# The entry of a fused encoder step: a smaller first chunk, the norm weight spread by TensorE, other loads and a written-out order

## Chip, core and metric

The kernel runs on one core of a Trainium2 chip. The core has TensorE (PE in the profile: matrix products, and transposes as products with an identity matrix), VectorE (DVE), ScalarE (ACT), GpSimd (POOL) and SyncE (SP, which here only issues loads and stores). Each engine takes its own instructions one after the other in a fixed order and waits for the others through counters (semaphores); ScalarE issues loads too. The metric is device time of one execution in microseconds (us).

## What is computed

One inference step of a hybrid encoder layer, for 1,024 prompt tokens and 32 sample tokens, 1,024 wide. Only its first part matters here: the norm of the tokens and the combined projection, whose columns feed three mixers (mLSTM, stick-breaking attention, S5).

```python
def layer(x, mem_k, mem_v, past_k, past_v, c0, n0, m0, s0_re, s0_im, conv_prev, prm):
    h = rmsnorm(x, prm['ln_mix_g'])
    z = h @ prm['w_in'] + prm['b_in']
    q_a, k_a, v_a, o_a, i_a, f_a, q_b, k_b, v_b, u_c = split_cols(z)
    ...
    x = x + y_mix @ prm['w_out']
    x = x + cross_attn(rmsnorm(x, prm['ln_x_g']), mem_k, mem_v, prm['w_xq'], prm['w_xo'])
    f, conv_new = conv_ffn(rmsnorm(x, prm['ln_ffn_g']), prm, conv_prev)
    ...
```

## The kernel before

**Split products.** Every f32 product is made of three on rounded operands (type fp32r): high part of the weights with high and low part of the tokens, low part of the weights with the high part of the tokens. The high part of a tile is a copy by ScalarE with rounding, the low part the difference, by VectorE or GpSimd.

**Token tiles.** `x_tile(i)` makes the normalised and transposed tokens of tile i, 128 tokens (tile 8 has the 32 of the sample). Its generator `norm_T` records: ScalarE squares and sums the tile; VectorE scales the sum and GpSimd takes its power -1/2; VectorE multiplies the tile by it and by the norm weights `gmix`, which must stand in all 128 partitions; and twice, for each half of the 1,024 columns: TensorE transposes four blocks into a PSUM tile `tp`, ScalarE copies it into `h_hi` (za and zb are the zones of `h_lo` and `h_hi`), VectorE makes the low part in `h_lo`.

**Projection.** `W` streams the weight tiles of 128 columns: `load` brings 512 KB, `split` makes `w_hi` and `w_lo`. The first three weight tiles are u0 and u1 (input of S5) and the gate, which has its high and low part side by side in one tile (zone zr) and so 16 products a chunk, where the others have 24. `dense_cmajor` runs these three chunk by chunk over the tokens (0 to 383, 384 to 767, 768 to 1055), so that TensorE has work before all tokens are there; `need_h(c)` holds a chunk back until its tiles are recorded. From the fourth weight tile on `dense` runs each tile over all chunks. `ev_in` evacuates each result by ScalarE.

**Order.** The Python code records instructions in the order of its own clock model, with side work (`vec_late` for later vectors, `s5`, `mlstm`, `stick`, the norm of the memory tokens) recorded between the products. A scheduler of the framework then sets each engine's order by its own estimate, within the dependences. It also gives every load one of eight counters; an issue waits until the load that had the counter before has landed. The first loads are issued by SyncE in this order, ahead of the bias vectors and the rest:

```python
        x_load(0, sy)
        sy.dma_start(gmix, a["ln_mix_g"][0].partition_broadcast(P))
        x_load(1, sy)
        x_load(2, sy)
        W.load()
        x_load(3, sy)
        W.load()
```

All instructions pass through one helper, so that the profile shows nearly all at line 173; tiles are told apart by names: zf and zy hold the loaded tokens and small vectors, mm is the PSUM tile of a product, gp one of small work.

Of the kernel before, what the change touches and what calls it, by code (L numbers as in the profile page):

```python
# [8 lines left out]
F32R = mybir.dt.float32r  # L9
# [31 lines left out]
IN_AT = [0, 3 * P, 6 * P, TA]  # L41


IN_W = max(IN_AT[c + 1] - IN_AT[c] for c in range(NCH))

# [8 lines left out]
def tile_fn(tc, *args):  # L54
# [77 lines left out]
    class Timed:  # L132
# [23 lines left out]
        def __getattr__(self, name):  # L156
# [17 lines left out]
            return timed  # L174

# [85 lines left out]
    with ExitStack() as top:  # L261
# [122 lines left out]
        class WStream:  # L384
# [21 lines left out]
            def split(self):  # L406
# [124 lines left out]
        sp = Bag({"ss": (4, 8), "stg": (3, IN_W), "sthl": (2, 2 * IN_W, "R"), "nat": (1, 9 * P)})  # L531
# [22 lines left out]
        def norm_T(src_ap, n, gB, hi, lo, t0, xt=None):  # L554
# [7 lines left out]
            s.activation(sq[:n], xt[:n].rearrange("p (k c) -> p k c", k=KD), AF.Square, accum_out=ss[:n, 0:1])  # L562
            yield
            v.tensor_scalar(ss[:n, 1:2], ss[:n, 0:1], 1.0 / D, EPS, op0=ALU.mult, op1=ALU.add)
            g.tensor_tensor(out=ss[:n, 2:3], in0=ss[:n, 1:2], in1=mhalf[:n], op=ALU.pow)
            yield
            v.scalar_tensor_tensor(xt[:n], xt[:n], ss[:n, 2:3], gB[:n], op0=ALU.mult, op1=ALU.mult)
            yield
            for q in range(2):
                ps = tp()  # L570
                for j in range(4):
                    k = 4 * q + j
                    pe.transpose(ps[:, j, :n], xt[:n, k * P:(k + 1) * P], ident[:n, :n])
                s.activation(hi[:, 4 * q:4 * q + 4, t0:t0 + n], ps[:, :, :n], AF.Copy)
                v.tensor_tensor(out=lo[:, 4 * q:4 * q + 4, t0:t0 + n], in0=ps[:, :, :n],
                                in1=asf(hi[:, 4 * q:4 * q + 4, t0:t0 + n]), op=ALU.subtract)
                yield
# [9 lines left out]
        def x_tile(i):  # L587
            yield from norm_T(None, P if i < 8 else TS, gmix, h_hi, h_lo, i * P, xts[i])
# [24 lines left out]
        sy.dma_start(bgate[0:4, :], a["b_in"][0, 1536:1540].unsqueeze(1))  # L613
        sy.dma_start(bgate[32:36, :], a["b_in"][0, 1540:1544].unsqueeze(1))
# [22 lines left out]
        def vec_late():  # L637
# [10 lines left out]
            yield  # L648
            pa, pb = gp(), gp()
            pe.transpose(pa[:, :34], ra[:34], ident[:34, :34])  # L650
            pe.transpose(pb[:, :88], rb, ident[:88, :88])
# [60 lines left out]
        def ev_in(jj, c, ps):  # L712
            key, j = order[jj]
            sl = slice(IN_AT[c], IN_AT[c + 1])
            w = IN_AT[c + 1] - IN_AT[c]
            rs_ = slice(j * P, (j + 1) * P)
            pv = ps[:, :w]
            if key == "u":
                if c == 0:
                    full[jj] = xb.tile([P, 8, NB], "ur")  # L720
                n0, nn = IN_AT[c] // 8, w // 8
# [8 lines left out]
            if key == "gate":  # L730

                sl_ = sp.tile([P, 3 * P], "stg")[:, :w]
# [16 lines left out]
            if key in ("qb", "kb"):  # L749
                hl = sp.tile([P, 2, IN_W], "sthl", F32R)[:, :, :w]  # L750
# [7 lines left out]
            if key in ("kb", "vb", "va", "oa"):  # L758
# [915 lines left out]

        hm = lambda k, c: (h_hi[:, k, IN_AT[c]:IN_AT[c + 1]], h_lo[:, k, IN_AT[c]:IN_AT[c + 1]])
        in_n = [IN_AT[c + 1] - IN_AT[c] for c in range(NCH)]
        chunks = list(range(NCH))
        h_free = []
        xw_ = add(Window((x_tile(i) for i in range(9)), 4))
        until(lambda: xn[0] >= 1)  # L1680
        W.prime(1)

        def need_h(c):
            until(lambda: xn[0] * P >= min(IN_AT[c + 1], T) and (c < 2 or xn[0] == 9))
# [19 lines left out]
        main = dense_cmajor(3, hm, chunks, in_n, ev_in, need_h)  # L1704
# [805 lines left out]
```

## Time and profile before

| | us |
|---|---|
| median of 3 runs | 1724.47 (1716.87 to 1728.94) |
| profiled execution | 1717.52 |
| its span, first to last instruction | 1715.7 |
| TensorE busy in the span | 1639.6 (96%) |

The span is what the rows below are counted from; 1.8 us lie around it. A timeline row has the start, the duration, the engine (q for its sequencer, which issues loads), line, operation, tiles, shapes, the number of merged instructions, and in brackets the idle time of the engine before it and what ended it. The end of a product is modelled, so that its duration overlaps that of the next; the pitch of their starts tells how fast they run.

### The profile page before, as it was taken

The numbers are of one execution on the slowest core, as the hardware profiler recorded it, in microseconds if no ns is written. First come the engines' busy times: TensorE is split into PE (matmuls) and PEld (weight loads), VectorE is DVE, ScalarE is ACT, GpSimd is POOL, SyncE is SP. The second block draws the span as 40 slices with busy tenths as digits, with TensorE's granted clock in tenths as the row PEclk, the third lists the DMA queues.
The fourth block names the chain that finished last, engine by engine and source line by source line (L and its number), as shares of the span: only waits on it lengthen the run. The fifth ranks groups of instructions, "written<-read, shape, count | busy, mean of one in ns | idle before, by whom it ended". The sixth has DMA issues, their size and how long they took to land.

```text
span 1715.7 us, 30436 instructions
## 1 busy us (share of the span) xinstructions
PE 1639.6 (96%) x11616; PEld 1595.5 (93%) x11616; DVE 1137.6 (66%) x2221; ACT 754.9 (44%) x1480; POOL 456.2 (27%) x612
## 2 busy tenths in 40 slices
PE   5999999999999899999999889999999999999997
PEld 5999989998899799999998889999999998999997
DVE  6788878745786657766656678877777777233232
ACT  5434534634665554544444534444444445111143
POOL 5234425011213333201102554333333330000022
PEclk9999999999999999999999989999999999999999
DMA  7464544254579874456653555322222227332111
GB/s 216 145 179 109 128 109 106 77 157 136 142 231 268 235 226 136 139 160 183 182 162 112 156 156 160 98 88 81 75 76 75 76 74 259 96 100 75 45 67 65
DMA packets 328391, 229.90 MB, mean 134 GB/s; under 512 B 43564, under 2 KB 309707, under 8 KB 327991
## 3 DMA queue, kind: packets, MB, share of 16 engines
q1 hardware_dynamic: 309991, 214.57, 42.6%
q10 hardware_dynamic: 18256, 13.40, 2.7%
q8 instruction: 92, 1.51, 0.4%
q14 instruction: 52, 0.43, 0.1%
HBM read 170.95 MB, written 56.38 MB: 133 GB/s over the span
## 4 chain that ended last, share of the span: by engine, by line
PE 76%; DVE 9%; DMA 9%; ACT 2%; issue 2%; POOL 2%; SPq 1%; ACTq 0%; DVEq 0%; POOLq 0%
PE mm L173 47%; PE gp L173 19%; PE tp L173 10%; DVE zy L173 3%; DVE zf L173 2%; DVE zx L173 2%; DMA out_dram<-zf 2%; DVE zr L173 1%; DVE w_lo L173 1%; POOL zf L173 1%; DMA zf<-d_act 1%; SPq L173 1%; POOL zy L173 1%; DMA d_mv<-zr 1%; DMA zf<-d_e 1%
## 5 line engine op out<-in xcount | busy, mean ns | idle before, releaser
L173 PE MATMUL mm<-zb,w_hi 128*128 128x352 f32 (+4 forms) x1234 | 365.2, 329 | 2.7 <-DVE zb L173 1.3
L173 PE MATMUL mm<-zr,w_hi 128*128 128x352 f32 (+2 forms) x1358 | 289.9, 313 | 6.3 <-DVE zx L173 2.8
L173 ACT ACTIVATE w_hi<-w_raw 128x1024 fp32r<-128x1024 f32 (+1 forms) x150 | 149.6, 997 | 284.8 <-PE mm L173 203.8
L173 PE MATMUL mm<-zb,w_lo 128*128 128x384 f32 (+2 forms) x826 | 272.4, 330 | 0.0
L173 POOL TENSOR_TENSOR zf<-zf 128x352 f32<-128x352 f32 (+5 forms) x98 | 117.4, 1200 | 578.4 <-ACT zf L173 493.2
L173 PE MATMUL mm<-zr,w_lo 128*128 128x264 f32 (+2 forms) x1058 | 236.2, 304 | 0.7 <-ACT zf L173 0.7
L173 PEld LDWEIGHTS mm<-zb,w_hi 128*128 128x128 f32 x1234 | 226.4, 189 | 4.7 <-DVE zb L173 1.6
L173 PEld LDWEIGHTS mm<-zr,w_hi 128*128 128x128 f32 x1358 | 217.2, 192 | 8.3 <-DVE zx L173 3.1
L173 DVE TENSOR_TENSOR w_lo<-w_raw,w_hi 128x1024 fp32r<-128x1024 f32 (+1 forms) x127 | 160.4, 1263 | 54.9 <-ACT w_hi L173 54.2
L173 DVE TENSOR_TENSOR zx<-mm,zx 128x352 f32<-128x352 f32 (+3 forms) x120 | 62.7, 523 | 186.1 <-PE mm L173 184.3
L173 PE MATMUL mm<-za,w_hi 128*128 128x384 f32 (+1 forms) x552 | 183.1, 332 | 0.0
L173 PEld LDWEIGHTS mm<-zr,w_lo 128*128 128x128 f32 x1058 | 164.7, 189 | 0.9 <-ACT zf L173 0.9
L173 PEld LDWEIGHTS mm<-zb,w_lo 128*128 128x128 f32 x826 | 156.5, 190 | 0.7
L173 PE MATMUL tp<-ident,zf 128*128 128x128 f32 (+3 forms) x530 | 89.2, 286 | 28.6 <-DVE zf L173 20.6
L173 PE MATMUL mm<-zy,w_hi 128*128 128x352 f32 x456 | 113.1, 324 | 1.6 <-DVE zx L173 1.6
L173 PE MATMUL gp<-zy 128*128 128x132 f32 (+13 forms) x722 | 109.8, 290 | 3.1 <-DVE zg L173 2.4
L173 DVE TENSOR_TENSOR zy<-zy 128x16 f32<-128x16 f32 (+9 forms) x371 | 97.3, 303 | 16.3 <-POOL zy L173 7.7
L173 ACT ACTIVATE zf<-gp 128x512 f32<-128x512 f32 (+6 forms) x180 | 75.6, 476 | 73.9 <-PE gp L173 57.1
L173 PEld LDWEIGHTS mm<-za,w_hi 128*128 128x128 f32 x552 | 105.6, 191 | 0.5
L173 PEld LDWEIGHTS gp<-zy 128*128 128x128 f32 (+6 forms) x722 | 97.3, 186 | 5.4 <-DVE zg L173 2.6
L173 PEld LDWEIGHTS tp<-ident,zf 128*128 128x128 f32 (+3 forms) x530 | 64.7, 146 | 38.2 <-DVE zf L173 19.2
L173 POOL TENSOR_TENSOR zy<-zy 128x16 f32<-128x16 f32 (+8 forms) x123 | 82.5, 682 | 64.4 <-DVE zy L173 54.6
(232 smaller groups left out, 3358.7 us busy)
## 6 DMA issues: line engine op xcount, KB each, us to landing
w_raw<-in_w_ffn_a_dram SPq DMA_DIRECT2D x27, 512.0 KB
w_raw<-in_w_out_dram SPq DMA_DIRECT2D x24, 512.0 KB
w_raw<-in_w_xq_dram SPq DMA_DIRECT2D x24, 512.0 KB
w_raw<-in_w_xo_dram SPq DMA_DIRECT2D x24, 512.0 KB
w_raw<-in_w_in_dram SPq DMA_DIRECT2D x23, 512.0 KB
d_act<-zx SPq DMA_DIRECT2D x22, 528.0 KB
zf<-d_act SPq DMA_DIRECT2D x22, 528.0 KB
w_raw<-in_w_ffn_down_dram SPq DMA_DIRECT2D x16, 512.0 KB
```

The lines of the kernel that those rows point to most:

```text
L173: return f(*args, **kw)
```

## The change

- The first three weight tiles run over chunks of 256, 384 and 416 tokens (`IN_FIRST`), the others over 384, 384 and 288 as before.
- The norm weight comes as one row of 4 KB through ScalarE's queue; two f32 products with a row of ones spread it over the partitions, and VectorE copies the result into `gmix`.
- The first weight tile is loaded ahead of token tile 2; bias and later vectors are issued by ScalarE (`rows`, `bgate`).
- `norm_T` multiplies each half of the columns right before that half's transposes.
- `pin` ties an instruction to the last pinned one of its engine, so that pinned instructions keep the order in which they are recorded. All ScalarE and VectorE instructions of `x_tile` and of the first three weight splits are pinned. The low parts of these splits go from GpSimd to VectorE.
- Tiles 0 and 1 are recorded by a written-out sequence; the transposes of `vec_late` wait for 8 us of the model's clock and keep the recorded order.

```diff
+IN_FIRST = [0, 2 * P, 5 * P, TA]
...
+    def pin(eng, name, *args, **kw):
+
+        if eng.key in pinned:
+            with tc.issue_after(pinned[eng.key]):
+                r = getattr(eng, name)(*args, **kw)
+        else:
+            r = getattr(eng, name)(*args, **kw)
+        pinned[eng.key] = r.ins
...
-                s.activation(hi[:, :kt, :cols], raw[:, :kt, :cols], AF.Copy)
-                (v if self.at + len(self.ready) > 2 else g).tensor_tensor(
-                    out=lo[:, :kt, :cols], in0=raw[:, :kt, :cols], in1=asf(hi[:, :kt, :cols]), op=ALU.subtract)
+                do = pin if self.at + len(self.ready) < 3 else free
+                do(s, "activation", hi[:, :kt, :cols], raw[:, :kt, :cols], AF.Copy)
+                do(v, "tensor_tensor", out=lo[:, :kt, :cols], in0=raw[:, :kt, :cols], in1=asf(hi[:, :kt, :cols]),
+                   op=ALU.subtract)
...
-            v.scalar_tensor_tensor(xt[:n], xt[:n], ss[:n, 2:3], gB[:n], op0=ALU.mult, op1=ALU.mult)
-            yield
             for q in range(2):
+                xh = xt[:n, 512 * q:512 * q + 512]
+                do(v, "scalar_tensor_tensor", xh, xh, ss[:n, 2:3], gB[:n, 512 * q:512 * q + 512], op0=ALU.mult,
+                   op1=ALU.mult)
                 ps = tp()
                 for j in range(4):
                     k = 4 * q + j
                     pe.transpose(ps[:, j, :n], xt[:n, k * P:(k + 1) * P], ident[:n, :n])
-                s.activation(hi[:, 4 * q:4 * q + 4, t0:t0 + n], ps[:, :, :n], AF.Copy)
-                v.tensor_tensor(out=lo[:, 4 * q:4 * q + 4, t0:t0 + n], in0=ps[:, :, :n],
-                                in1=asf(hi[:, 4 * q:4 * q + 4, t0:t0 + n]), op=ALU.subtract)
+                do(s, "activation", hi[:, 4 * q:4 * q + 4, t0:t0 + n], ps[:, :, :n], AF.Copy)
+                do(v, "tensor_tensor", out=lo[:, 4 * q:4 * q + 4, t0:t0 + n], in0=ps[:, :, :n],
+                   in1=asf(hi[:, 4 * q:4 * q + 4, t0:t0 + n]), op=ALU.subtract)
                 yield
...
+        grow = xts[7][0:1, :]
+        s.dma_start(grow, a["ln_mix_g"][0].unsqueeze(0))
         x_load(0, sy)
-        sy.dma_start(gmix, a["ln_mix_g"][0].partition_broadcast(P))
         x_load(1, sy)
+        W.load()
         x_load(2, sy)
         W.load()
         x_load(3, sy)
-        W.load()
+        for q in range(2):
+            pq = gp()
+            pe.matmul(pq, ones4[0:1, :], grow[:, 512 * q:512 * q + 512], start=True, stop=True)
+            v.tensor_copy(gmix[:, 512 * q:512 * q + 512], pq)
...
-        xw_ = add(Window((x_tile(i) for i in range(9)), 4))
-        until(lambda: xn[0] >= 1)
+
+        first = [x_tile(i) for i in range(2)]
+        for x in first:
+            next(x)
+            next(x)
+        for _ in first[0]:
+            pass
+        next(first[1])
         W.prime(1)
+        for _ in first[1]:
+            pass
+        add(Window((x_tile(i) for i in range(2, 9)), 2))
```

VectorE's first instructions before, from its first one on: SCALAR_TENSOR_TENSOR is the multiplication of a tile, TENSOR_TENSOR za the low part of a half (tp with its number is the half), TENSOR_SCALAR zf a tile's statistic.

```order
L173 TENSOR_SCALAR zf_87<-zf_87 128x1
L173 TENSOR_SCALAR zy_91<-zy_91 128x128
L173 SCALAR_TENSOR_TENSOR zf_87<-zf_87 128x1024
L173 TENSOR_TENSOR zy_91<-zy_91,ident_114 16x256
L173 TENSOR_SCALAR zf_87<-zf_87 128x1
L173 SCALAR_TENSOR_TENSOR zf_87<-zf_87 128x1024
L173 TENSOR_SCALAR zf_87<-zf_87 128x1
L173 TENSOR_TENSOR za_75<-tp_193,zb_79 128x4x128
L173 SCALAR_TENSOR_TENSOR zf_87<-zf_87 128x1024
```

VectorE with the change, from tile 0's first low part (tp_190) to the second weight tile's low part; 64x256, 128x128 and 16x256 are operations of S5 on loaded parameters, the last of them on `ssm_d`.

```order
L175 TENSOR_TENSOR za_75<-tp_190,zb_79 128x4x128
L175 SCALAR_TENSOR_TENSOR zf_87<-zf_87 128x512
L175 TENSOR_TENSOR za_75<-tp_198,zb_79 128x4x128
L175 SCALAR_TENSOR_TENSOR zf_87<-zf_87 128x512
L175 TENSOR_TENSOR za_75<-tp_206,zb_79 128x4x128
L175 TENSOR_TENSOR w_lo_214<-w_raw_130,w_hi_213 128x1024
L175 SCALAR_TENSOR_TENSOR zf_87<-zf_87 128x512
L175 TENSOR_SCALAR zy_91<-zy_91 64x256
L175 TENSOR_SCALAR zy_91<-zy_91 128x128
L175 TENSOR_TENSOR zy_91<-zy_91,ident_114 16x256
L175 TENSOR_TENSOR za_75<-tp_218,zb_79 128x4x128
L175 TENSOR_TENSOR w_lo_230<-w_raw_133,w_hi_229 128x1024
```

Before, two tiles are multiplied ahead of the first low part; now multiplication and low part of a half take turns, and S5's operations stand ahead of tile 1's last low part.

ScalarE around the same place with the change: zb is the copy of a transposed half, DMA a load that it issues; the three last rows ahead of w_hi_229 are two S5 loads and the copy of tile 1's second half.

```order
L175 ACTIVATE zb_79<-tp_198 128x4x128
L175 DMA zy_91<-in_ffn_conv_w_dram 22x128
L175 DMA zy_91<-in_ffn_conv_b_dram 22x128
L175 DMA zy_91<-in_ssm_c_im_dram 128x64
L175 ACTIVATE zb_79<-tp_206 128x4x128
L175 ACTIVATE w_hi_213<-w_raw_130 128x1024
L175 DMA zy_91<-in_ssm_c_re_dram 128x64
L175 DMA zy_91<-in_ssm_d_dram 16x256
L175 ACTIVATE zb_79<-tp_218 128x4x128
L175 ACTIVATE w_hi_229<-w_raw_133 128x1024
```

Before, ScalarE's loads of S5 stand ahead of all its copies and it issues none between them. In the built program `ssm_d` has the counter of an `ssm_b_im` load, which SyncE issues after all token tiles.

TensorE before, in chunk 1 (384 columns): tp_318 and tp_336 are halves of later token tiles, mm_329 the sum of the second weight tile, mm_378 that of the gate.

```order
L173 MATMUL mm_329<-za_75,w_hi_259 128x384
L173 MATMUL tp_318<-ident_114,zy_91 128x128 x4
L173 MATMUL mm_329<-zb_79,w_lo_260 128x384
L173 MATMUL mm_329<-zb_79,w_hi_259 128x384
L173 MATMUL mm_329<-za_75,w_hi_259 128x384
L173 MATMUL mm_329<-zb_79,w_lo_260 128x384
L173 MATMUL tp_336<-ident_114,zy_91 128x128 x4
L173 MATMUL mm_378<-zb_79,zr_83 128x384
```

TensorE with the change, from the end of chunk 1 to chunk 2 (416 columns): tp_404 is tile 5's second half, tp_512 the first of tile 8, the two gp rows are the transposes of `vec_late`.

```order
L175 MATMUL tp_404<-ident_114,zy_91 128x128 x4
L175 MATMUL gp_413<-ident_114,zy_91 128x34
L175 MATMUL gp_414<-ident_114,zy_91 128x88
L175 MATMUL tp_426<-ident_114,zy_91 128x128 x4
L175 MATMUL tp_447<-ident_114,zy_91 128x128 x4
L175 MATMUL tp_471<-ident_114,zy_91 128x128 x4
L175 MATMUL tp_493<-ident_114,zy_91 128x128 x4
L175 MATMUL tp_512<-ident_114,zy_91 128x32 x4
L175 MATMUL mm_543<-zb_79,w_hi_213 128x416
```

Before, transposes of later tiles stand between products; now six halves follow each other with no product between them.

## Rows read from the trace of the kernel before

**Rows 1.** The page, busy time of each engine.

```profile
PE 1639.6 (96%) x11616; PEld 1595.5 (93%) x11616; DVE 1137.6 (66%) x2221; ACT 754.9 (44%) x1480; POOL 456.2 (27%) x612
```

**Rows 2.** Windows: stretch, length, busy us by engine, granted clock, DMA share, GB/s.

```profile
0.00:20.00 20.00, 4.62 (x16) 2.86 (x16) 10.21 (x15) 11.32 (x18) 14.16 (x40) 1.00 0.84 252
20.00:36.73 16.73, 14.38 (x84) 13.65 (x85) 11.87 (x22) 9.64 (x19) 7.35 (x8) 1.00 0.89 246
...
64.03:114.00 49.97, 49.04 (x315) 47.97 (x314) 43.77 (x230) 17.13 (x31) 11.07 (x31) 1.00 0.67 187
114.00:664.00 550.00, 523.09 (x3714) 496.64 (x3713) 401.45 (x741) 284.30 (x637) 157.61 (x245) 0.98 0.58 161
```

**Rows 3.** Timeline of TensorE in the entry.

```profile
16.58 1.01 PE L173 MATMUL mm<-zb,w_hi 128*128 128x384 f32 x2 [1.17 <-ACT zb L173]
...
20.00 2.79 PE L173 MATMUL tp<-ident,zf 128*128 128x128 f32 x12 [2.41 <-DVE zf L173]
...
36.73 0.42 PE L173 MATMUL mm<-zb,zr 128*128 128x384 f32 x1 [0.87 <-ACT zy L173]
...
64.03 0.33 PE L173 MATMUL mm<-zb,w_hi 128*128 128x384 f32 x1
```

**Rows 4.** Timeline: loads, and what their landing releases.

```profile
4.99 1.06 ACT L173 ACTIVATE za<-zf 128x1024 fp32r<-128x1024 f32 x1 [2.31 <-DMA zf<-in_x_prompt_dram]
5.20 0.33 SPq L173 DMA_DIRECT2D zf<-in_x_prompt_dram  x1
...
5.95 0.19 ACT L173 ACTIVATION_READ_ACCUMULATOR za<-zf 128x1 f32 x1
...
14.98 1.06 ACT L173 ACTIVATE w_hi<-w_raw 128x1024 fp32r<-128x1024 f32 x1 [0.43 <-DMA w_raw<-in_w_in_dram]
...
23.83 0.40 SPq L173 DMA_DIRECT2D w_raw<-in_w_in_dram  x1
```

**Rows 5.** ScalarE's evacuation of the gate, its loads; VectorE's low weight part (groups, 26 to 64).

```profile
40.25 0.57 ACT L173 ACTIVATE zf<-mm,bgate 4x384 f32<-4x384 f32 x1 [0.81 <-PE mm L173]
...
45.73 0.43 ACTq L173 DMA_DIRECT2D zy<-in_state_ssm_re_dram  x1
...
47.15 0.28 ACT L173 ACTIVATE zb<-tp 128x128 fp32r<-128x128 f32 x1 [2.90 <-DMA zy<-in_state_ssm_re_dram]
...
L173 DVE TENSOR_TENSOR w_lo<-w_raw,w_hi 128x1024 fp32r<-128x1024 f32 x2 | 2.4, 1222 | 0.0
```

**Rows 6.** Timeline: the operations of a token tile.

```profile
9.82 0.57 POOL L173 TENSOR_TENSOR zf<-zf,mhalf 128x1 f32<-128x1 f32 x1 [2.31 <-DVE zf L173]
...
13.77 1.11 PE L173 MATMUL tp<-ident,zf 128*128 128x128 f32 x4 [0.90 <-DVE zf L173]
...
13.97 0.58 ACT L173 ACTIVATE zb<-tp 128x512 fp32r<-128x512 f32 x1
...
14.58 0.69 DVE L173 TENSOR_TENSOR za<-tp,zb 128x512 fp32r<-128x512 f32 x1 [0.33 <-ACT zb L173]
...
24.67 1.28 DVE L173 SCALAR_TENSOR_TENSOR zy<-zy,zf 128x1024 f32<-128x1024 f32 x1
...
27.33 0.60 PE L173 MATMUL tp<-ident,zf 128*128 128x128 f32 x4
```

**Rows 7.** Timeline of TensorE: starts of products, at both levels and both chunk widths.

```profile
23.23 0.50 PE L173 MATMUL mm<-zb,w_hi 128*128 128x384 f32 x1
...
23.55 0.38 PE L173 MATMUL mm<-za,w_hi 128*128 128x384 f32 x1
...
24.12 0.34 PE L173 MATMUL mm<-za,w_hi 128*128 128x384 f32 x1
...
26.02 0.34 PE L173 MATMUL mm<-za,w_hi 128*128 128x384 f32 x1
...
55.21 0.29 PE L173 MATMUL mm<-zb,w_hi 128*128 128x288 f32 x1
...
61.47 0.29 PE L173 MATMUL mm<-zb,w_lo 128*128 128x288 f32 x1
```

More of the change, by code (lines that the diff above doesn't have):

```diff
@@ L41 @@
 IN_AT = [0, 3 * P, 6 * P, TA]
-IN_W = max(IN_AT[c + 1] - IN_AT[c] for c in range(NCH))
+IN_FIRST = [0, 2 * P, 5 * P, TA]
+IN_W = max(at[c + 1] - at[c] for at in (IN_AT, IN_FIRST) for c in range(NCH))
+IN_HL = 3 * P
 REORDER = 15.0
@@ L174, in __getattr__, with free @@
             return timed
+    pinned = {}
+    def pin(eng, name, *args, **kw):
[5 more added lines that the diff above has]
+        pinned[eng.key] = r.ins
+    def free(eng, name, *args, **kw):
+        getattr(eng, name)(*args, **kw)
     v = Timed(nc.vector, "dve")
@@ L552, in gain_rows, with norm_T @@
             yield
-        def norm_T(src_ap, n, gB, hi, lo, t0, xt=None):
+        def norm_T(src_ap, n, gB, hi, lo, t0, xt=None, do=free):
             if xt is None:
@@ L647, in vec_late @@
             rows(rb, at, a["ffn_conv_b"][0])
-            yield
+            t = clk["pe"]
+            while clk["pe"] < t + 8:
+                yield
             pa, pb = gp(), gp()
-            pe.transpose(pa[:, :34], ra[:34], ident[:34, :34])
-            pe.transpose(pb[:, :88], rb, ident[:88, :88])
+            tc.keep_in_program_order(pe.transpose(pa[:, :34], ra[:34], ident[:34, :34]))
+            tc.keep_in_program_order(pe.transpose(pb[:, :88], rb, ident[:88, :88]))
             v.tensor_copy(vecC, pa[:, :34])
@@ L730, in ev_in @@
             if key == "gate":
-                sl_ = sp.tile([P, 3 * P], "stg")[:, :w]
+                sl_ = sp.tile([P, IN_W], "stg")[:, :w]
                 for r0 in (0, 32):
@@ L749, in ev_in @@
             if key in ("qb", "kb"):
-                hl = sp.tile([P, 2, IN_W], "sthl", F32R)[:, :, :w]
+                hl = sp.tile([P, 2, IN_HL], "sthl", F32R)[:, :, :w]
                 s.activation(hl[:, 0], st, AF.Copy)
@@ L1672, in glu, with hm, in_n @@
             yield
-        hm = lambda k, c: (h_hi[:, k, IN_AT[c]:IN_AT[c + 1]], h_lo[:, k, IN_AT[c]:IN_AT[c + 1]])
-        in_n = [IN_AT[c + 1] - IN_AT[c] for c in range(NCH)]
+        def hm(at):
+            return lambda k, c: (h_hi[:, k, at[c]:at[c + 1]], h_lo[:, k, at[c]:at[c + 1]])
+        def in_n(at):
+            return [at[c + 1] - at[c] for c in range(NCH)]
         chunks = list(range(NCH))
         h_free = []
-        xw_ = add(Window((x_tile(i) for i in range(9)), 4))
-        until(lambda: xn[0] >= 1)
+        first = [x_tile(i) for i in range(2)]
[5 more added lines that the diff above has]
+        next(first[1])
         W.prime(1)
+        for _ in first[1]:
+            pass
+        add(Window((x_tile(i) for i in range(2, 9)), 2))
         def need_h(c):
-            until(lambda: xn[0] * P >= min(IN_AT[c + 1], T) and (c < 2 or xn[0] == 9))
+            until(lambda: xn[0] * P >= min(IN_FIRST[c + 1], T) and (c < 2 or xn[0] == 9))
         def lend():
@@ L1703, in tile_fn @@
         vec_cols()
-        main = dense_cmajor(3, hm, chunks, in_n, ev_in, need_h)
+        main = dense_cmajor(3, hm(IN_FIRST), chunks, in_n(IN_FIRST), ev_in, need_h)
         n_main = 0
@@ L1710, in tile_fn @@
                 later_sides()
-        drive(dense(len(order) - 3, hm, chunks, in_n, lambda j, c, ps: ev_in(j + 3, c, ps)))
+        drive(dense(len(order) - 3, hm(IN_AT), chunks, in_n(IN_AT), lambda j, c, ps: ev_in(j + 3, c, ps)))
         clear(0)
```

23 lines of the change are left out of this document (12 added, 11 removed).

## The prediction

> **What bounds the kernel now.** The page comes first: TensorE is busy for 96% of the span [rows 1], so a microsecond in which it lacks work is mostly a microsecond of the end time. The busy time by stretches then says where it lacks work [rows 2]: it is busy for 4.62 of the first 20 us and 14.38 of the next 16.73, so 17.7 us are idle there, but only 0.9 us between 64 and 114, and 27 us in the 550 us that follow. The entry is the largest hole. TensorE's timeline shows what ends its waits there [rows 3]: the first product, at 16.58, waits for ScalarE's copy of a transposed tile, the transposes at 20.00 for VectorE's normalised tile, and at 36.73 for ScalarE once more. My marker is the first product of the fourth weight tile, at 64.03 [rows 3]: by then all three chunks of the first three weight tiles are done. Whatever the change does to the entry must show there.
>
> **Loads.** The weight row leaves SyncE's queue, and with it 512 KB that went out second. From 4.99, when the first token tile lets ScalarE start, to 14.98, when the second weight tile does, six transfers of 512 KB land [rows 4], 1.67 us each. Tile 1 takes the row's place and lands at about 6.65; all that follows comes 1.67 us sooner. The 4 KB row goes through ScalarE's queue instead. No row shows such a load; the nearest is ScalarE's first load of before, whose landing releases SyncE's issue at 5.20 [rows 4]. Two f32 products and two copies spread the row; I give them until 8 to 9, which is when VectorE is free for tile 0 anyway: tile 1's square and sum take 1.15 us as tile 0's do, 4.99 to 6.14 [rows 4], so from 6.65 to 7.8, and VectorE's small operation on them stands ahead of tile 0's first half, so the halves start at about 8.2 at best. The vectors that went through SyncE now go through ScalarE's sequencer, 15 issues of about 0.4 us between its copies [rows 5]. By row that is no free place: ScalarE stood idle for 2.90 us behind its own loads [rows 5]. The Trainium skill ("DMA: Bandwidth & Descriptors", section "Issuing engines are not separate DMA queues") says that spreading loads over engines saves only the issuing time, since all run on the same 16 engines; by that SyncE's saving is all that the move has, and by the row ScalarE pays for it.
>
> **The norm, in halves that wait for each other.** Before, VectorE has the next tile's multiplication between a tile's multiplication and its two low parts, so transposes and copies run meanwhile. Now its order is: half a tile's multiplication, then that half's low part, then the next half. The low part needs TensorE's four transposes and ScalarE's copy of them, so VectorE waits for the whole round. A round is 0.70 for half of 1.28 and its start-up, transposes 1.11 or 0.60, the copy 0.58, the low part 0.69 [rows 6], less 0.07 of overlap and plus 0.13 in three handovers: 3.15 or 2.65. The two durations of the same four transposes are TensorE's two levels, 1.2 and 2.4 GHz: 1.11 while it had done little but wait, 0.60 after a run of products; the granted clock of the windows reads 1.00 in both [rows 2], so the durations decide. The Trainium skill ("TensorE: Matmul & The Clock Gate", Part 1) says that the clock falls back after idling; by that every round with nothing but transposes would cost 3.15, by the faster row 2.65, which for eleven rounds is 5.5 us of difference. I take 3.15 up to the second low weight part and 2.65 after it.
>
> **The sum to the marker.** (a) Tile 0's two halves and tile 1's first: 8.2 + 3 x 3.15 = 17.65. ScalarE's high weight part (1.06, as at 14.98 [rows 4]) follows its last copy: 18.0, which is the first product, 1.4 later than before. The low weight part moves from GpSimd to VectorE, where it takes 1.22 [rows 5]: 19.3. Ahead of it VectorE has nothing, behind it wait tile 1's second half and ten products. A product of 384 columns starts every 0.32 at the low level and every 0.173 (11 in 1.90) later; 288 columns 0.133 (47 in 6.26) [rows 7]. By the same slope 256 columns are 0.213 or 0.120 and 416 are 0.187. So the first half of the sum over k ends at 21.4, the transposes at 22.5.
> (b) Three S5 operations now stand on VectorE ahead of tile 1's last low part. One waits for `ssm_d`, whose issue stands on ScalarE ahead of the last copy and waits for an `ssm_b_im` load (same counter). That load is behind tile 7, which landed at 23.83 before (SyncE's issue there waits for it [rows 4]), so at 22.2 now; with two small loads it lands at about 23.3, `ssm_d` 2 to 4.4 us later, I take 26.0 with its issue. VectorE: 0.4 for the S5 operation, 0.69 for the low part: 27.1. Eleven products at 0.213 end at 29.5. Second low weight part: 28.4.
> (c) Tile 2's statistics and power (0.57 and handovers) let its first half start at 29.2; its transposes stand behind 21 products (32.0); low part 34.0. Second half 36.6; the gate's low part, also moved to VectorE, 37.3; 16 gate products 39.2. The gate's four evacuations (0.57 for 384 columns [rows 5], about 0.44 for 256) are ahead of tile 3's copy: 41.0. Tile 3's halves 42.3 and 45.0, tile 4's power 0.95, its first half 48.6. Only then chunk 1 runs: 20 products 52.1, a round's rest for tile 4's second half 54.0, 24 products 58.1, gate 61.3.
> (d) For chunk 2 TensorE's order has nothing but transposes between chunk 1's gate and its first product: six rounds, tile 5's second half to tile 8's first. Gate evacuation 63.4, tile 5 64.7, tiles 6 and 7 each 0.95 + 5.3: 77.2, tile 8 80.0. Then 48 products of 0.187, a break of 1.3 and 16 gate products: 93.
> So the marker moves from 64 to 93, 29 us later. The products themselves are as many and cost the same: 0.120 + 0.173 + 0.187 = 0.48 against 2 x 0.173 + 0.133. The bounds: fast transposes in (a) and S5 loads 2 us sooner, halves at their best and the handovers hidden, give 83; slow transposes in (c) and (d) and 4.4 us for each small load give 101. That is +19 to +37.
>
> **After the marker** TensorE has 0.9 us of slack in 50 us and about 27 in the next 550 [rows 2]. Most of these waits are for work that itself hangs on the projection, so they shift with it. I take off 4, bounds 0 and 14. The listing is also reshuffled further down; the first pieces of later stages stand in other places, for which I have no price but a few us either way. Net +25, bounds +5 to +37. The profiled execution took 1717.52, so it would be 1742.5. The median of the three runs is 1724.47, 7 above it; I put the forecast on the median: 1749.
>
> **Rivals.** First, the slack takes it (not slower). Waits between 64 and 664 add up to 28 us, as much as the delay. If they belong to chains that don't start from the projection (loads, the sequential S5 and attention work on VectorE), TensorE would reach them later and not wait: 1717 to 1728. It decides from 12 us absorbed on. For it: VectorE is as busy as 43.77 of 50 us between 64 and 114 [rows 2]. Against: the S5 preparation stands behind the norm on VectorE and starts late too.
> Second, the change does what it says. If the halves overlap after all and chunk 0 starts at 15 without the wait at 20.00, the holes before 16.58 and at 20.00 and 36.73 [rows 3] shrink by some 6 us: 1718 on the median, within 1%. Against: VectorE has no instruction to run between a half's two operations.
> Third, rounds at about 2.2 and no wait for `ssm_d`: eleven rounds less 0.45 and 3 us less give +17 at the end, 1741, the edge of 1%.
> Fourth, more waits: each of ScalarE's issues needs the landing of the load that had its counter before. If small loads take 4.4 us, as the one of before beside full traffic [rows 4], tile 0's copies wait too: +35, 1760.
>
> **How the numbers follow.** Forecast with its two neighbours above 1% (1742 to 1760): 0.77. The slack takes it, or most: 0.11. It works as said: 0.08, of which 0.03 above 1% faster. Third rival below 1%: 0.04. 1% is 17 us here, about what a measurement of this kernel can tell from no change, as the three runs lie 12 us apart. Slower 0.77, same 0.20, faster 0.03. The range must hold 8 in 10: the low end is the sum's lower bound on the median, 1729, less 3 for the lower profiled execution; the high end is +37.
>
> **What would show it.** Right: the first 384-column product at about 48, the first 416-column one at about 80, the fourth weight tile at about 93; VectorE idle before nearly every low part of a token tile, released by ScalarE; transposes alone on TensorE for some 15 us. Right for (b): VectorE waiting for `ssm_d` near 24 to 26. Wrong: the fourth weight tile before 75, or the 1% reached with the marker late, which would mean that the slack took it.

## The result and the profile after

The changed kernel takes 1797.91 us (median of 4 runs, 1796.32 to 1799.00) against 1721.12 for the kernel before: 1.0447 times as long, 95% interval 1.0418 to 1.0475. The direction was forecast, the size was not: +77 where +25 was said.

The page of the changed kernel, two lines (they answer to [rows 1]; the second is the granted clock in 40 slices, in tenths):

```profile
PE 1672.8 (93%) x11620; PEld 1619.3 (90%) x11620; DVE 1145.3 (64%) x2237; ACT 762.7 (43%) x1485; POOL 440.8 (25%) x609
...
PEclk8699999999988889999999999999999999999999
```

As many products as before but for four, 33 us more busy time and 46 us more idle time. The clock line says where to look: the first 90 us, and slices 12 to 15. The fourth weight tile starts at 106.76 and not at 64.03 [rows 3], so the profile is cut there, at the projection's last product (464.8 and 514.0) and at the issue of the 57th weight load, one of w_out (664.9 and 747.0). Windows of the changed kernel, columns as in [rows 2]:

```profile
0.00:20.00 20.00, 7.93 (x19) 3.99 (x19) 6.98 (x14) 6.49 (x10) 6.64 (x34) 1.00 0.87 270
20.00:36.73 16.73, 10.63 (x58) 9.62 (x58) 5.51 (x12) 5.34 (x10) 1.07 (x2) 0.90 0.60 151
36.73:52.62 15.89, 6.78 (x28) 5.66 (x29) 5.75 (x11) 6.49 (x13) 0.65 (x2) 0.53 0.06 19
52.62:73.67 21.05, 16.29 (x79) 14.95 (x79) 7.14 (x14) 5.99 (x11) 1.62 (x3) 0.82 0.00 1
73.67:89.92 16.25, 4.97 (x20) 3.35 (x20) 5.86 (x12) 5.99 (x11) 1.64 (x3) 0.50 0.01 3
89.92:106.80 16.88, 16.88 (x79) 15.87 (x80) 8.68 (x28) 4.47 (x7) 6.11 (x7) 0.82 0.33 98
106.80:514.00 407.20, 390.95 (x2621) 371.48 (x2619) 301.31 (x735) 181.92 (x367) 112.46 (x217) 0.98 0.47 129
514.00:747.00 233.00, 200.79 (x1414) 189.53 (x1413) 152.22 (x263) 130.90 (x314) 59.60 (x70) 0.90 0.70 202
747.00:1794.50 1047.50, 1017.59 (x7310) 1004.89 (x7308) 651.89 (x1155) 415.10 (x743) 250.98 (x274) 0.99 0.37 116
```

The same three later stretches of the kernel before:

```profile
64.03:464.80 400.77, 390.34 (x2658) 371.02 (x2657) 299.91 (x718) 186.46 (x380) 109.56 (x215) 0.99 0.48 128
464.80:664.90 200.10, 182.68 (x1377) 174.49 (x1376) 146.19 (x253) 115.36 (x289) 59.93 (x62) 0.97 0.81 231
664.90:1715.70 1050.80, 1020.30 (x7310) 1007.72 (x7309) 653.03 (x1154) 416.12 (x746) 255.52 (x278) 0.99 0.37 115
```

So the 78.8 us between the two profiles fall in two parts: 42.7 before the fourth weight tile, and 36 behind it, of which 6.4 in the rest of the projection, 32.9 from its end to the 57th load, -3.3 in the rest. Between the fourth tile and the 57th load both kernels run the same number of instructions on TensorE (4035 each). Of 600.9 us before, 27.8 are idle and 11.9 are lost to the low level (one minus the granted clock, summed over windows of 5 us); of 640.2 us after, 48.5 and 30.8. What is left is 561.2 and 561.0: the work is the same, and the whole loss is waiting plus the low level that comes with it. Idle time at the low level counts in both terms, so this is an account and no exact split; over all runs below it closes to 8 us.

TensorE's timeline of the changed kernel in the entry:

```profile
8.38 1.11 PE L175 MATMUL tp<-ident,zf 128*128 128x128 f32 x4 [1.55 <-DVE zf L175]
12.80 1.12 PE L175 MATMUL tp<-ident,zf 128*128 128x128 f32 x4 [3.30 <-DVE zf L175]
15.99 1.12 PE L175 MATMUL tp<-ident,zf 128*128 128x128 f32 x4 [2.07 <-DVE zf L175]
18.85 0.58 PE L175 MATMUL mm<-zb,w_hi 128*128 128x256 f32 x1 [1.75 <-ACT w_hi L175]
...
27.75 0.58 PE L175 MATMUL mm<-za,w_hi 128*128 128x256 f32 x1 [2.76 <-DVE za L175]
...
38.51 0.55 PE L175 MATMUL mm<-zb,zr 128*128 128x256 f32 x1 [2.10 <-DVE zr L175]
...
52.62 1.01 PE L175 MATMUL mm<-zb,w_hi 128*128 128x384 f32 x2 [0.69 <-ACT zb L175]
...
54.15 0.52 PE L175 MATMUL mm<-zb,w_hi 128*128 128x384 f32 x1
54.47 0.52 PE L175 MATMUL mm<-za,w_hi 128*128 128x384 f32 x1
...
73.67 1.11 PE L175 MATMUL tp<-ident,zy 128*128 128x128 f32 x4 [4.33 <-DVE zy L175]
76.95 1.09 PE L175 MATMUL tp<-ident,zy 128*128 128x128 f32 x4 [2.16 <-DVE zy L175]
81.61 1.08 PE L175 MATMUL tp<-ident,zy 128*128 128x128 f32 x4 [3.58 <-issue]
...
89.92 1.06 PE L175 MATMUL mm<-zb,w_hi 128*128 128x416 f32 x2 [0.37 <-ACT zb L175]
...
106.76 0.34 PE L175 MATMUL mm<-zb,w_hi 128*128 128x384 f32 x1
```

VectorE's in the same stretch, low parts and what they wait for, and at the end the way from a tile's low part to the next tile (statistic, then multiplication):

```profile
11.39 0.69 DVE L175 TENSOR_TENSOR za<-tp,zb 128x512 fp32r<-128x512 f32 x1 [2.99 <-ACT zb L175]
...
14.58 0.69 DVE L175 TENSOR_TENSOR za<-tp,zb 128x512 fp32r<-128x512 f32 x1 [1.84 <-ACT zb L175]
...
26.68 0.41 DVE L175 TENSOR_TENSOR zy<-zy,ident 16x256 f32<-16x256 f32 x1 [1.54 <-DMA zy<-in_ssm_d_dram]
27.03 0.67 DVE L175 TENSOR_TENSOR za<-tp,zb 128x512 fp32r<-128x512 f32 x1
...
79.87 0.15 DVE L175 TENSOR_SCALAR zf<-zf 128x1 f32<-128x1 f32 x1 [0.48 <-ACT za L175]
80.76 0.75 DVE L175 SCALAR_TENSOR_TENSOR zy<-zy,zf 128x512 f32<-128x512 f32 x1 [0.73 <-POOL zf L175]
```

The rounds stand in series: transposes, then ScalarE's copy, then VectorE's low part, and only then the next half's multiplication, 3.2 to 3.3 us from a tile's first round to its second (12.80 to 15.99, 73.67 to 76.95) and 4.7 from there to the next tile's first (76.95 to 81.61).

ScalarE's copy of tile 0's first half starts 1.3 us after the transposes end (9.49), released by the landing of a load:

```profile
10.76 0.60 ACT L175 ACTIVATE zb<-tp 128x512 fp32r<-128x512 f32 x1 [3.69 <-DMA zy<-in_ln_f_g_dram]
```

### The profile page after: what moved, and what is told of

The parts are those of the page before. It is cut to its first block, busy times and chain, and to the rows that moved or that the text cites. A ratio compares the mean times of both kernels' runs of the same rounds, so it can differ in the third digit from the quotient of the medians.

```text
span 1794.5 us, 30504 instructions
## 1 busy us (share of the span) xinstructions
PE 1672.8 (93%) x11620; PEld 1619.3 (90%) x11620; DVE 1145.3 (64%) x2237; ACT 762.7 (43%) x1485; POOL 440.8 (25%) x609
## 4 chain that ended last, share of the span: by engine, by line
PE 71%; DVE 11%; DMA 10%; ACT 3%; issue 2%; POOL 1%; SPq 0%; ACTq 0%; DVEq 0%; POOLq 0%
PE mm L175 45%; PE gp L175 16%; PE tp L175 9%; DVE zy L175 4%; DVE zf L175 2%; DVE zx L175 2%; DVE zr L175 2%; DVE w_lo L175 1%; DMA zf<-d_t 1%; DMA w_raw<-in_w_out_dram 1%; ACT L175 1%; POOL zy L175 1%; DMA zy<-d_uu 1%; DMA zf<-d_e 1%; ACT zf L175 1%
## 5 line engine op out<-in xcount | busy, mean ns | idle before, releaser
L175 PE MATMUL mm<-zb,w_lo 128*128 128x384 f32 (+4 forms) x826 | 275.6, 334 | 0.5 <-DVE w_lo L175 0.5
L175 DVE TENSOR_TENSOR w_lo<-w_raw,w_hi 128x1024 fp32r<-128x1024 f32 x129 | 160.6, 1246 | 62.7 <-ACT w_hi L175 62.4
L175 PE MATMUL mm<-za,w_hi 128*128 128x384 f32 (+3 forms) x552 | 186.2, 337 | 2.9 <-DVE za L175 2.8
L175 DVE TENSOR_TENSOR zy<-zy 128x16 f32<-128x16 f32 (+8 forms) x377 | 101.9, 313 | 30.3 <-POOL zy L175 11.4
L175 PE MATMUL gp<-zy 128*128 128x132 f32 (+13 forms) x722 | 113.4, 296 | 3.8 <-issue 2.9
L175 PE MATMUL tp<-ident,zf 128*128 128x128 f32 (+2 forms) x530 | 89.1, 286 | 23.2 <-DVE zf L175 13.3
L175 PEld LDWEIGHTS tp<-ident,zf 128*128 128x128 f32 (+2 forms) x530 | 63.9, 146 | 32.4 <-DVE zf L175 10.7
```

The lines of the kernel that those rows point to most:

```text
L175: return f(*args, **kw)
```

## The experiments

"Fourth tile" is the start of the fourth weight tile, "behind it" the span less that time, "gates" how long after the fourth tile the mLSTM's gate preparation is stored (the issue of `d_uu`), all from the profiles; the ratio is to the kernel before on the same chip. Before: 64.0, 1651.7, 360.6. The profiled execution of the kernel before, 1717.5, is one of its faster ones; its medians beside these runs are 1721.1 to 1724.3. So differences to before in "behind it" are mostly some us larger than by the medians (median of the run less that of before, less the difference at the fourth tile), by up to 10; the medians' figure is given beside them below.

| run | median us | ratio (95%) | fourth tile | behind it | gates |
|---|---|---|---|---|---|
| changed kernel | 1797.9 | 1.0447 (1.0418 to 1.0475) | 106.8 | 1687.7 | 394.1 |
| free_all | 1756.3 | 1.0203 (1.0173 to 1.0234) | 65.5 | 1688.4 | 395.6 |
| whole | 1756.3 | 1.0197 (1.0163 to 1.0232) | 79.2 | 1681.5 | 379.7 |
| window4 | 1789.3 | 1.0406 (1.0373 to 1.0439) | 105.9 | 1681.4 | 356.3 |
| same_chunks | 1791.2 | 1.0404 (1.0372 to 1.0436) | 106.6 | 1684.7 | 380.6 |
| after_warm | 1787.5 | 1.0375 (1.0344 to 1.0406) | 104.5 | 1682.6 | 391.4 |
| pin_only | 1740.2 | 1.0112 (1.0084 to 1.0140) | 70.3 | 1666.0 | 366.2 |
| halves_only | 1735.6 | 1.0086 (1.0057 to 1.0116) | 62.6 | 1671.2 | 366.3 |
| chunks_only | 1729.0 | 1.0037 (1.0020 to 1.0054) | 63.1 | 1663.6 | 366.0 |
| loads_only | 1722.7 | 0.9998 (0.9981 to 1.0016) | 64.0 | 1659.3 | 362.6 |
| whole_free | 1740.3 | 1.0110 (1.0078 to 1.0142) | 68.2 | 1668.3 | 377.4 |
| reorder14 | 1732.7 | 1.0082 (1.0051 to 1.0113) | 63.7 | 1667.1 | 360.1 |
| free_s0 | 1742.4 | 1.0106 (1.0088 to 1.0124) | 66.6 | 1672.6 | 376.4 |
| after_s0 | 1782.5 | 1.0333 (1.0316 to 1.0351) | 104.7 | 1676.3 | 375.4 |
| before_late | 1754.4 | 1.0169 (1.0151 to 1.0187) | 63.7 | 1688.3 | 421.4 |
| before_early | 1747.0 | 1.0147 (1.0118 to 1.0176) | 63.2 | 1681.1 | 374.6 |
| loads_s0 | 1748.7 | 1.0165 (1.0127 to 1.0204) | 64.6 | 1677.5 | 360.3 |

**free_all.** The changed kernel with nothing pinned.

```diff
-            yield from norm_T(None, P if i < 8 else TS, gmix, h_hi, h_lo, i * P, xts[i], pin)
+            yield from norm_T(None, P if i < 8 else TS, gmix, h_hi, h_lo, i * P, xts[i])
...
-                do = pin if self.at + len(self.ready) < 3 else free
+                do = free
```

> The changed kernel with nothing pinned: everything is recorded in the same order, but the framework's scheduler may set VectorE's and ScalarE's order again, and it then puts the multiplications of later tiles ahead of the low parts. Theory A (the pinned order makes each half tile a round in series, and the entry's loss of 41 us up to the fourth weight tile is that): the fourth weight tile starts at 65 to 75 instead of 104. For the second loss of some 38 us, in the end of the projection and beside the memory tokens' products: theory B (it comes from another order of the listing further down, whatever the entry does) says that it stays, so about 1755 to 1770; theory C (it follows from the entry's lateness, as the mixers' work reaches the end of the projection too late) says that it goes too, so 1715 to 1735. Rival D (loads and the small first chunk cost the entry its time, not the pin): the fourth weight tile stays at 95 or later and the time above 1780.

The entry's loss goes but for 1.5 us (65.5), and what is behind the fourth tile stays, to 1 us (34 us by the medians in both kernels). That settles two things: the entry's loss is the pinned order, and the later loss doesn't come from the entry's lateness. Windows of this run: the early stretch is whole again, the last one is as long as the changed kernel's, at 0.88 of the clock.

```profile
0.00:65.50 65.50, 52.91 (x282) 46.94 (x283) 39.02 (x93) 35.29 (x64) 21.48 (x52) 0.95 0.57 153
65.50:472.70 407.20, 389.94 (x2621) 369.86 (x2620) 299.07 (x730) 180.45 (x364) 106.55 (x214) 0.99 0.47 128
472.70:704.90 232.20, 202.01 (x1416) 191.70 (x1415) 152.69 (x263) 128.27 (x313) 58.49 (x70) 0.88 0.71 203
```

VectorE in this run, two multiplications of halves together and a low part that waits for nothing:

```profile
14.25 1.41 DVE L175 SCALAR_TENSOR_TENSOR zf<-zf 128x512 f32<-128x512 f32 x2
...
16.24 0.68 DVE L175 TENSOR_TENSOR za<-tp,zb 128x512 fp32r<-128x512 f32 x1
```

**whole, window4, same_chunks, pin_only: which part of the pinned order.** The first three each take one part back in the changed kernel: tiles multiplied whole; four tiles at a time in place of two; the old chunks. The fourth is the kernel before with its own recorded order pinned.

```diff
-            for q in range(2):
-                xh = xt[:n, 512 * q:512 * q + 512]
-                do(v, "scalar_tensor_tensor", xh, xh, ss[:n, 2:3], gB[:n, 512 * q:512 * q + 512], op0=ALU.mult,
-                   op1=ALU.mult)
+            do(v, "scalar_tensor_tensor", xt[:n], xt[:n], ss[:n, 2:3], gB[:n], op0=ALU.mult, op1=ALU.mult)
+            yield
+            for q in range(2):
```

> The changed kernel with the pinned order kept, but each token tile multiplied whole, ahead of its two halves, as before. Theory A (a half's multiplication stands behind the other half's low part, which makes the rounds serial): TensorE gets a tile's two rounds of transposes at once and its order has products between them again, so most of the 41 us go: fourth weight tile at 70 to 85. Rival (the pin alone is enough to put the rounds in series): 95 to 104. For the end, theory B (second loss independent of the entry) 1755 to 1790, theory C (it follows the lateness) 1725 to 1750.

```diff
-        add(Window((x_tile(i) for i in range(2, 9)), 2))
+        add(Window((x_tile(i) for i in range(2, 9)), 4))
```

> The changed kernel with four token tiles at a time from tile 2 on, as before, in place of two; halves and pins stay. VectorE's order is still a half's multiplication, that half's low part, and so on. Theory A: the rounds stay in series, fourth weight tile at 95 to 108, time 1770 to 1800. Rival (the window of two is what keeps the tiles apart): 70 to 85, 1740 to 1770.

```diff
-IN_FIRST = [0, 2 * P, 5 * P, TA]
+IN_FIRST = [0, 3 * P, 6 * P, TA]
```

> The changed kernel with the old chunks of 384, 384 and 288 tokens for the first three weight tiles; pin and halves stay. Theory A: the rounds are in series as before, so the fourth weight tile comes at 95 to 110 and the time is 1785 to 1810. Rival (the narrow first chunk, which leaves TensorE with less work per round, is what costs): 75 to 85, and 1740 to 1770.

```diff
...
-            v.scalar_tensor_tensor(xt[:n], xt[:n], ss[:n, 2:3], gB[:n], op0=ALU.mult, op1=ALU.mult)
+            do(v, "scalar_tensor_tensor", xt[:n], xt[:n], ss[:n, 2:3], gB[:n], op0=ALU.mult, op1=ALU.mult)
...
-            yield from norm_T(None, P if i < 8 else TS, gmix, h_hi, h_lo, i * P, xts[i])
+            yield from norm_T(None, P if i < 8 else TS, gmix, h_hi, h_lo, i * P, xts[i], pin)
```

> The kernel before with ScalarE's and VectorE's instructions of the token tiles pinned to the order in which they are recorded there: whole tiles, four at a time, so that the multiplications stand ahead of the low parts. Theory A (the harm is in what is pinned, half and low part in turn, not in pinning): fourth weight tile at 62 to 70. Rival (any pin forces the rounds apart): 80 or later. The recording behind it is that of before: if the recording sets the later loss, the stretch from the fourth weight tile to the end takes 1650 to 1662 as before and the time is 1717 to 1730; if the scheduler's placing is enough, 1665 to 1690 and 1735 to 1755.

In the entry neither the window nor the chunks matter (105.9, 106.6). With halves the pin costs 41 us (106.8 against 65.5 without it), with whole tiles 11 (79.2 against 68.2 in whole_free, below): a tile's two rounds go to TensorE at once. Pinning the old order costs 6, and its fourth weight tile at 70.3 lies just outside theory A's range. VectorE there does four multiplications ahead of the first low part, at 22.75; the third, which chunk 0 needs, ends at 20.6, and the first product comes at 22.5 (16.58 before). Three of them (VectorE's timeline, pin_only):

```profile
14.19 6.42 DVE L173 SCALAR_TENSOR_TENSOR zf<-zf 128x1024 f32<-128x1024 f32 x3
```

So it is mostly the content of the order that costs: a half's multiplication behind the other half's low part. What ScalarE's pins and VectorE's cost apart was not tested. Behind the fourth tile pin_only is 14 us longer than before (12 by the medians), though by its edit its recording is that of before: the scheduler's placing alone is enough to lose there.

**after_warm: is it TensorE's level?** The changed kernel with products in the gaps.

```diff
                 ps = tp()
+                for j in range(12 if t0 >= 3 * P and hi is h_hi else 0):
+                    with tc.issue_after(pinned["warm"]):
+                        pinned["warm"] = nc.tensor.matmul(ps.rearrange("p a b -> p (a b)")[:, :2 * P], h_hi[:, j % KD, 0:P], h_hi[:, j % KD, 0:2 * P], start=True, stop=True).ins
...
```

> The changed kernel with twelve products of 256 columns added ahead of each half's four transposes from token tile 3 on; their results are overwritten by the transposes, so nothing that is computed changes. They wait for nothing but a free PSUM tile and stand where TensorE waits for VectorE (2.2 to 3.6 us a round). Theory F (of the 14 us by which the entry's loss exceeds the forecast, nearly all is TensorE at its low level after the waits: rounds of 3.3 for 2.65, 416-column products at 0.347 for 0.187): the granted clock of the stretch from 52 to 105 is near 1.00, the transposes take 0.60, and the fourth weight tile starts at 92 to 99 instead of 106.8, though 1.3 us of products were added to each round. Rival G (the rounds are bound by VectorE, ScalarE and GpSimd and by nothing of TensorE's level): 106 to 115. The end moves with it as far as the listing behind it stays: 1780 to 1795 by F.

Neither theory hit. Two views of this run, its windows and TensorE's timeline:

```profile
70.00:90.00 20.00, 13.06 (x82) 11.80 (x82) 8.66 (x17) 6.42 (x12) 2.19 (x4) 0.85 0.04 10
```

```profile
72.74 0.66 PE L175 MATMUL tp<-ident,zy 128*128 128x128 f32 x4 [2.88 <-DVE zy L175]
...
75.47 1.12 PE L175 MATMUL tp<-ident,zy 128*128 128x128 f32 x4
...
80.12 0.66 PE L175 MATMUL tp<-ident,zy 128*128 128x128 f32 x4 [1.73 <-DVE zy L175]
...
86.74 0.43 PE L175 MATMUL tp<-ident,zy 32*128 32x32 f32 x4 [1.60 <-DVE zf L175]
87.10 2.58 PE L591 MATMUL tp<-zb 128*128 128x256 f32 x12
...
90.11 1.02 PE L175 MATMUL mm<-zb,w_hi 128*128 128x416 f32 x2
```

The level was raised: in the entry the low level now takes 5.1 us and not 23.9, and a round after faster transposes takes 2.7 to 3.0 (72.74 to 75.47, 80.12 to 83.07). But a tile still takes 6.6 to 7.4 us (7.3 to 7.9 in the changed kernel) and TensorE still waits for VectorE: the chain through the four engines sets the pace, its transposes at the low level only some 0.5 of each round. The added products also cost time of their own. The groups at 57.08 and 63.10 stand among chunk 1's products, where they cost 1.5 each (to the next product at 58.58 and 64.60). The one at 87.10 keeps TensorE busy until 89.61, though ScalarE's copy, which chunk 2's first product waits for in the changed kernel, ends at 87.48:

```profile
87.20 0.28 ACT L175 ACTIVATE zb<-tp 128x128 fp32r<-128x128 f32 x1 [0.79 <-PE tp L175]
```

That is 2.1 us more. Without the three groups the fourth tile would have come at about 99.4 by these numbers, an estimate, and the lifted level would have won some 7 of the 14 us that the entry lost beyond the forecast. So the level is about half of it: F's "nearly all" is not borne out, nor is G's nothing.

**Single parts.** loads_only is the kernel before with the new order of loads, the spread weight row and ScalarE's vectors; halves_only and chunks_only have one part each; whole_free is the changed kernel without pins and with whole tiles.

```diff
...
         x_load(0, sy)
-        sy.dma_start(gmix, a["ln_mix_g"][0].partition_broadcast(P))
         x_load(1, sy)
+        W.load()
         x_load(2, sy)
...
-            sy.dma_start(tl[at:at + n, :], ap.rearrange("(r c) -> r c", c=P))
+            s.dma_start(tl[at:at + n, :], ap.rearrange("(r c) -> r c", c=P))
```

> The kernel before with one part of the change alone: the weight row spread by TensorE, the new order of loads and the vectors issued by ScalarE; old chunks, nothing pinned, whole tiles multiplied. By the prediction's own step the loads give 1.67 us less for each transfer behind the row, and ScalarE's issues take it back: fourth weight tile at 61 to 66. By theory E the listing has the mLSTM even some 16 us of the model's clock earlier than before, so 1705 to 1730 in the end. Rival D (the vectors on ScalarE cost the entry much): fourth weight tile at 72 or later.

```diff
-            v.scalar_tensor_tensor(xt[:n], xt[:n], ss[:n, 2:3], gB[:n], op0=ALU.mult, op1=ALU.mult)
-            yield
             for q in range(2):
+                xh = xt[:n, 512 * q:512 * q + 512]
+                v.scalar_tensor_tensor(xh, xh, ss[:n, 2:3], gB[:n, 512 * q:512 * q + 512], op0=ALU.mult, op1=ALU.mult)
```

> The kernel before with each half of a token tile multiplied right before its transposes, nothing pinned. Theory A: the scheduler sets the multiplications ahead again, fourth weight tile at 62 to 70. If the recording sets the later loss, this one changes it and the stretch from the fourth weight tile to the end takes 10 to 40 us more than before's 1652: 1725 to 1765. If halves cost nothing anywhere, 1715 to 1727.

```diff
...
-        main = dense_cmajor(3, hm, chunks, in_n, ev_in, need_h)
+        main = dense_cmajor(3, hm(IN_FIRST), chunks, in_n(IN_FIRST), ev_in, need_h)
```

> The kernel before with the chunks of 256, 384 and 416 tokens for the first three weight tiles alone. The first product has to wait for two tiles in place of three: first product at 14 to 17, fourth weight tile at 60 to 66. For the later loss as for the halves: 1720 to 1760 if the recording sets it, 1713 to 1725 if not.

> The changed kernel without the pins and with whole tiles multiplied: what is left is the small first chunk, the spread weight row, the loads and the written-out start. Theory A: fourth weight tile at 58 to 66, as the rounds overlap. Theory E: the listing has the mLSTM's gate preparation 338 us of the model's clock behind the fourth weight tile, 10 more than before, so 1715 to 1735. Rival: the small chunk costs the entry something by itself, fourth weight tile at 70 or later.

The loads are worth nothing, as the sum had it. Halves and chunks alone win 1.4 and 0.9 us in the entry and lose 20 and 12 behind it (15 and 8 by the medians). whole_free is 4 us later at the fourth tile and 17 longer behind it (15 by the medians): at 68.2 it lies between theory A's range and the rival's, and its time is above theory E's.

**What sets the later loss.** reorder14 leaves the entry as it is and shifts the recording a little. The five others move the start of the mLSTM, which is recorded only after S5 has left its memory, by the slack of S5's steps (loads_s0 on top of loads_only).

```diff
-REORDER = 15.0
+REORDER = 14.0
```

> The kernel before with one constant of the recording's clock model changed from 15 to 14: the entry is the same to the instruction, and the order differs only from the end of the projection on. Theory B (the order there is a matter of luck, worth tens of us): the time differs from before by 10 to 40 us either way with the fourth weight tile at 64 as before. Theory C: within 6 us of before, as nothing is late.

```diff
-SLACK = [-0.25, 1, -0.5]
+SLACK = [0, 1, -0.5]
```

> The kernel with nothing pinned and one number of the recording changed: the S5 steps are recorded as soon as the clock model has their inputs (slack 0) and not 0.25 us later. In the listing this puts the mLSTM's gate preparation, which is recorded only after S5 has left its memory, at the same distance behind the fourth weight tile as before the change (about 33 us of the model's clock earlier than in the unpinned kernel). Theory E (the second loss is S5's four rounds being listed further apart by the change, so that the mLSTM starts some 33 us later and lies beside the memory tokens' products, where TensorE waits for it): 1720 to 1738. Theory B (any other listing is a matter of luck): 1745 to 1770, no nearer to before than the unpinned kernel's 1756.

> The changed kernel, pins and all, with the slack of S5 at 0. Theory E: the entry's loss of 41 us stays, the fourth weight tile at about 104, and the second loss goes for the most part: 1760 to 1775. Theory B: 1785 to 1810. Rival C (the entry's lateness itself lengthens the later part): 1785 to 1800 too, with the mLSTM starting earlier after the fourth weight tile and nothing won.

```diff
-SLACK = [-0.25, 1, -0.5]
+SLACK = [-0.4, 1, -0.5]
```

> The converse: the kernel before, its entry the same to the instruction, with the slack of S5 at -0.4, so that the listing has the mLSTM's start some 42 us of the model's clock further back. Theory E: the fourth weight tile at 64 as before, the mLSTM's gates written 35 to 45 us later, and the time 1745 to 1765. Theory B: 1700 to 1740, by luck. If it is within 1% of before although the gates come 40 us later, theory E falls.

```diff
-SLACK = [-0.25, 1, -0.5]
+SLACK = [0.25, 1, -0.5]
```

> The kernel before with the slack of S5 at 0.25, which lists the mLSTM's start 7 us of the model's clock earlier. Theory E: 1708 to 1724, a little faster than before if anything, the fourth weight tile at 64. Theory B (luck): anything from 1705 to 1745.

> The kernel with the loads part alone and the slack of S5 at 0, which lists the mLSTM's start 16 us of the model's clock earlier than before. Theory E: 1700 to 1718, faster than before. Theory B: 1710 to 1745, no relation to where the mLSTM starts.

The row that stands for the gates, first in the kernel before, then in before_late, SyncE's queue:

```profile
424.58 0.25 SPq L173 DMA_DIRECT2D d_uu<-zy  x1
```

```profile
485.10 0.25 SPq L173 DMA_DIRECT2D d_uu<-zy  x1
```

Theory E holds in the direction it was built for: gates 60 us later cost 36.6 behind an unchanged entry (30 by the medians), and gates 18 to 19 us sooner give 11 to 16 back in the unpinned and the pinned kernel, about half of what was expected. It fails as the whole cause: loads_s0, reorder14 and window4 have the gates where before has them, or sooner, and are 26, 15 and 30 us longer behind the fourth tile (27, 12 and 25 by the medians). before_early does not test it: its gates were to come 7 us sooner and came 14 later. Theory B (luck) is what remains, but it is not shown: free_all, whole and reorder14 lie in its ranges, free_s0, after_s0, before_late, before_early and loads_s0 outside them. The seventeen other listings give 1659 to 1688 behind the fourth tile. By the medians sixteen of them are slower than before, by 7 to 77 us in all, and loads_only is as fast, so not every other order costs. No version that ran beats the kernel before. In all eighteen the stretch from the fourth tile to the 57th load is 556 to 564 us plus its idle time plus the low level; only these two differ by more.

## Why the prediction was wrong

- **Loads and (a), (b): right, (a) in part by luck.** First product 18.85 for 18.0. VectorE waits for `ssm_d` until 26.68 (forecast 26.0) and ends the low part at 27.70 (27.1 by the sum). In (a) two errors work against each other: the halves start at 7.58 and not at 8.2, and tile 0's first copy waits 1.3 us for a load (10.76). The loads alone are worth nothing (loads_only).
- **The serial norm: right in kind.** Fifteen of the eighteen low parts wait for ScalarE, and six halves' transposes follow each other on TensorE with no product between them; free_all takes all but 1.5 of the entry's 42.7 us back.
- **(c) and (d): sized too small.** Chunk 1 came at 52.62 for 48.6, chunk 2 at 89.92 for 80, the marker at 106.76 for 93. The step that failed is "I take 3.15 up to the second low weight part and 2.65 after it" and the products at the high level. Tile 2's round took 2.72 (33.06 to 35.78), but later ones with no product between them 3.2 to 3.3: behind the second low weight part seven sets of transposes ran at 1.05 to 1.11 and not at 0.60, some 3.4 us. From a tile's second round to the next tile's first it took 4.66, 1.4 more than a round's 3.28, where 0.95 was counted for the power: VectorE also waits 0.48 for ScalarE's square (79.87). The 16 gate products of chunk 0 ran at 0.213 in place of 0.120, the first 17 of chunk 1 at 0.32 in place of 0.173, the first 15 of chunk 2 at 0.347 in place of 0.187 (92.17 to 92.52): 6.4 us. The granted clock is 0.53 and 0.50 in the two stretches of rounds. The Trainium skill ("TensorE: Matmul & The Clock Gate", Part 1) says that the clock falls back after idling; the trace agrees with it (73.67: transposes of 1.11 behind 4.33 us of idle time; 65.12, between products: 0.60). By after_warm the level is worth some 7 of the 14, an estimate; how the rest divides stays open.
- **After the marker: the step that failed most.** "I take off 4, bounds 0 and 14", with "no price but a few us either way" for the reshuffled listing. Measured: +36 (34 by the medians). Nothing of the delay was absorbed, as free_all, which is on time, takes as long behind the marker. The new listing lost 21 us of waits and 19 of low level between the fourth tile and the 57th load. The slack of 28 us that the prediction saw there was not a reserve; it was the least that any of the listings had in its profile (31.7 to 49.1 in the others).
- **Rivals.** The first (slack) and the second (as said) are refuted by the marker and the span, the third by rounds of 3.2. The fourth had the wait for loads right (ScalarE stands idle for 5.16 us ahead of its copy at 23.96), but most of the time came from elsewhere. That a new listing could cost tens of us was no rival at all, and it carries 40 of the 54 us of error in the profiles' terms (36 for -4), the entry the other 14.
- **Open:** which property of a listing decides. The mLSTM's start moves it, but two listings with nearly equal starts, before and loads_s0, differ by 26 us. What was seen in single cases (below) doesn't sort all eighteen.

## What to carry to other kernels

An order written out by hand must not follow one tile through the engines: on an engine that takes its instructions in order, put the next tile's independent work ahead of the step that waits for the round trip. Where a recorder or a scheduler sets the order of everything that follows, an edit at the entry is two edits; cut the profile at a marker behind the edit and judge both parts apart, and learn the second one's spread from a harmless change of the recording (here, by the medians, 12 us for one constant and 8 and 15 for parts that win 1). Price a wait of TensorE as the wait plus the low level behind it: over the later stretch 21 us more idle came with 19 more of low level.

## What the runs showed of the hardware

In the rows below ScalarE loads its function table at every change between exponentials and sigmoids, 1.28 us each, and two mixers that share ScalarE make it change at every turn. In the changed kernel the mLSTM's exponentials (zy) and the sigmoids of the stick attention (zf from gp) alternate beside the memory tokens' products; ScalarE's timeline:

```profile
531.05 1.28 ACT L175 ACT_TABLE_LOAD   x1
532.35 0.30 ACT L175 ACTIVATE zy<-gp 128x96 f32<-128x96 f32 x2
532.67 1.28 ACT L175 ACT_TABLE_LOAD   x1
533.96 1.08 ACT L175 ACTIVATE zf<-gp 128x512 f32<-128x512 f32 x2
535.06 1.28 ACT L175 ACT_TABLE_LOAD   x1
536.36 0.69 ACT L175 ACTIVATE zy<-zy 128x128 f32<-128x128 f32 x2
537.07 1.28 ACT L175 ACT_TABLE_LOAD   x1
```

The window there shows ScalarE as the busy one, TensorE idle for 3.9 us (2.7 of it behind ScalarE) and at 0.83:

```profile
530.00:550.00 20.00, 16.09 (x109) 14.33 (x108) 8.80 (x15) 19.34 (x38) 2.67 (x5) 0.83 0.29 76
```

Between the projection's end and the 57th load the changed kernel has eight loads of a table, before has one. It is no rule for the later loss, since after_s0 and window4 have one there too and still lose.
